# A two-layer hybrid decoder trunk: weight squares between an output group's high parts, squares behind the third tile's copies at the layer boundary, and another hand-written order for the first tiles

## The chip, the cores and the metric

One core of a Trainium2 chip. The metric is the device time of one execution in microseconds (us). TensorE (PE) multiplies matrices; VectorE (DVE), ScalarE (ACT) and GpSimd (POOL) do the rest; SyncE (SP) issues most DMA transfers.

## The reference

Two layers; the input is 512 tokens of width 2048 in float32. Each layer normalises, projects once to all branches, runs three branches and projects their concatenation back:

```python
def _layer(x, norm_g, w_in, conv_w, conv_b, sb_qn_g, sb_kn_g, gla_w_up, gla_b_up, gla_on_g, w_out):
    h = _rmsnorm(x, norm_g).astype(x.dtype)
    proj = h @ w_in
    (cv_h, cv_b, cv_c, cv_g, sb_q, sb_k, sb_v, sb_g,
     gl_q, gl_k, gl_v, gl_g, gl_lr) = jnp.split(proj, split_points, axis=-1)
    y_conv = _short_conv(cv_h, cv_b, cv_c, conv_w, conv_b) * jax.nn.silu(cv_g.astype(f32))
    ...  # y_sb: stick-breaking attention on q, k, v; y_gla: gated linear attention in chunks of 64
    mix = jnp.concatenate([y_conv, y_sb, y_gla], axis=-1).astype(x.dtype)
    return x + mix @ w_out
```

`w_in` is 2048 x 7696 and `w_out` 2048 x 2048 in each layer, both float32. The changed places belong to `_rmsnorm` and `h @ w_in` (the first tiles and the layer boundary) and to `x + mix @ w_out` (the output groups).

## The kernel before

**Numbers in two parts.** Every float32 operand of a product is scaled by a power of two and split into two float16 parts, a high one and a low one (what the high one left), and a product is three matmuls: high by high, high by low, low by high. The activations are `mix`, two constant tiles (`act` in the rows), 128 rows by 16 slices of the width by 4 token tiles.

**Weight groups.** Weights are worked on in groups of 256 columns; the list `specs` has them in the order of use, and `i` is a group's place in it. For each group:
- `fetch` (L332 issues the DMAs on SP) brings two staged float32 halves, `st`, of 1 MB each. There are four such buffers, so two groups are staged at a time.
- `wmax` takes the sum of squares of each half on ACT (L344, 128x2048, result into `wm`, kept in the dictionary `peak`; the instruction in `squares`).
- `wscale` sums over the partitions on POOL (L357, into `wgm`) and works out the scale on DVE (L359 to L371, `ws` the scale, `wu` its inverse). POOL and these DVE steps run only once the second square is there.
- Either `whi`/`wlo` write four quarters, a high part on ACT (L419, with L417 for a group that has 16 more columns) and a low part on DVE (L423); or, where `modes[i]` is set, `right` writes the seven right operands of a two-by-two product with seven instead of eight block products: seven high parts on ACT (L436) and seven low parts on DVE (L437), and between them four DVE sums of staged blocks (L440, L441, L444, L445), for which later high parts wait. The result tiles are `w`, of which the pool has six.
- `weights()` hands a group to its user, issues `fetch(i + 2)` and calls `load(i + 1)`, so a group is prepared while the one before it is multiplied.

In `load_` the two squares of group i are put, in ACT's order, behind the second high part of group i - 1. `tc.issue_after(x)` is a hint for the scheduler: the enclosed instructions stand behind x in their engine's queue. Everything else outside the hand-written stretch is placed by a scheduler that simulates the kernel; `tc.high_priority()` moves work ahead of what else is ready. The instructions of each engine are then run in that order.

**Output groups.** `w_out` has eight groups in each layer. In layer 0, groups 2 to 6 go through `seven`, group 7 through `project_by_token` (matmuls L653); in layer 1, groups 2 to 7. `seven` multiplies seven products of 48 matmuls each (L680, 128x128), of which the first needs the first high and low part of the group, the second the second and so on (product order 0, 1, 3, 2, 4, 5, 6). Its results are combined on ACT (L691) and DVE (L1380 to L1402) with the residual, and in layer 0 ACT squares them for the next layer's norm (`square`, L1348).

**The first tiles.** Up to L620 or so the order of DVE and ACT is written by hand (`tc.manual_schedule`): the lines of calls stand in the order in which both engines run them. For each of four token tiles of 128 rows: `xsquare` (ACT, L547) sums the squares of its input; `xnorm` works out the factor (L198, L199 on ACT, L201 to L205 and L495 on DVE); `xgain` multiplies (DVE, L501, one for each half); `xhigh` transposes eight 128x128 blocks on PE (L513) and copies the result as the high part (ACT, L515); `xlow` makes the low part, either by a DVE subtract (L522) or by two PE matmuls with the negative identity (L525) and a copy on ACT (L526). Group 0's quarters are `whi0` (high parts: ACT L407 or DVE L409) and `wlo` (L423). PE's first products (L653) use the first tiles as they come.

**The layer boundary.** The last output group of layer 0 is done by token tile, and each finished tile goes straight into layer 1's preparation, `xprep`: tiles 0 and 1 by split copies and transposing transfers on SP, tiles 2 and 3 by `xhigh` and `xlow`. In the same stretch the first weight groups of layer 1 are prepared.

Of the kernel before, what the change touches and what calls it, by code (L numbers as in the profile page):

```python
# [10 lines left out]
AF = mybir.ActivationFunctionType  # L11
# [28 lines left out]
def hybrid_trunk(ctx, tc, x, norm_g, w_in, conv_w, conv_b, sb_qn_g, sb_kn_g,  # L40
# [3 lines left out]
    depth, D = norm_g.shape  # L44
# [28 lines left out]
    def sm(n, tag, bufs=None):  # L73
        return small.tile([P, n], F32, tag=tag, name=nm(tag), bufs=bufs)
# [117 lines left out]
        V.tensor_scalar(c.bitcast(I32), c.bitcast(I32), 0x7F800000, None, ALU.bitwise_and)  # L192
        V.tensor_scalar(dst, c, 2.0 ** lift, None, ALU.mult)

    def rsqrt(dst, src, scale, n, tag):

        r0 = sm(n, tag + "r0")
        S.activation(r0, src, AF.Ln, scale=scale, bias=epst)  # L198
        S.activation(r0, r0, AF.Exp, scale=-0.5)  # L199
        m = sm(n, tag + "rm")  # L200
        V.tensor_scalar(m, src, scale, EPS, ALU.mult, ALU.add)  # L201
        t = sm(n, tag + "rt")
        V.scalar_tensor_tensor(t, r0, -0.5, r0, ALU.mult, ALU.mult)
        V.tensor_tensor(t, t, m, ALU.mult)
        V.scalar_tensor_tensor(dst, t, 1.5, r0, ALU.add, ALU.mult)  # L205

    identb = const.tile([P, P], BF16, tag="identb", name="identb")
    V.tensor_copy(identb, ident)
# [81 lines left out]
    specs = []  # L290
# [49 lines left out]
    def wmax(i, h):  # L340

        if h == 0:
            peak[i] = sm(2 + len(specs[i][2]) // 2, "wm")
        squares[i] = S.activation(junk(HK * GW).rearrange("p (k n) -> p k n", k=HK), staged[i][h], AF.Square,  # L344
                                  accum_out=peak[i][:, h:h + 1])
        if h and len(specs[i][2]) > 1:
            S.activation(junk(KT * LR).rearrange("p (k n) -> p k n", k=KT), staged[i, 2], AF.Square,
                         accum_out=peak[i][:, 2:3])
# [53 lines left out]
    def whi0(h, q, eng):  # L402

        wtile(0)
        hi = quarter(0, 2 * h + q, 0)
        if eng is S:
            S.activation(hi, staged4(0, 2 * h + q), AF.Copy, scale=scales[0])  # L407
        else:
            V.tensor_scalar(hi, staged4(0, 2 * h + q), scales[0], None, ALU.mult)  # L409
# [18 lines left out]
    def right(i):  # L428

        a, b = (staged[i][0][:, :, c * P:(c + 1) * P] for c in range(2))  # L430
        c, d = (staged[i][1][:, :, c * P:(c + 1) * P] for c in range(2))

        def part(x):
            w = wtile(i)
            hi, lo = (w[:, h, :HK * P].rearrange("p (k n) -> p k n", n=P) for h in range(2))
            his.setdefault(i, []).append(S.activation(hi, x, AF.Copy, scale=scales[i]))  # L436
            V.scalar_tensor_tensor(lo, x, scales[i], hi, ALU.mult, ALU.subtract)  # L437

        part(a)
        V.tensor_tensor(b, b, d, ALU.add)  # L440
        V.tensor_tensor(a, a, b, ALU.add)  # L441
        part(a)
        part(c)
        V.tensor_tensor(c, c, a, ALU.add)  # L444
        V.tensor_tensor(a, a, d, ALU.subtract)  # L445
        part(a)
        part(b)
        part(d)
        part(c)

    def load_(i):

        with tc.issue_after(his[i - 1][min(1, len(his[i - 1]) - 1)].ins):
            for h in range(2):
                wmax(i, h)
        wscale(i)
        if modes[i]:
            right(i)
            return
        for q in range(4):  # L460
            whi(i, q)
            wlo(i, q)
# [23 lines left out]
    def xnorm(l, t):  # L486

        tot = ssq[:, t, 0:1]
        if l:
            tot = sm(1, "xtot")  # L490
            V.tensor_reduce(tot, ssq[:, t, :], AX.X, ALU.add)
        rstd = sm(1, "xrstd")
        rsqrt(rstd, tot, 1.0 / D, 1, "x")
        rs_ = sm(1, "xrs")
        V.tensor_tensor(rs_, rstd, xsc[:, l:l + 1], ALU.mult)  # L495
        xscale[t] = rs_
# [6 lines left out]
            V.scalar_tensor_tensor(xv[:, n:], tail[0][:, t, :], xscale[t], gb[h][:, n:], ALU.mult, ALU.mult)  # L503

    xps = {}

    def xhigh(t, h, dst):

        xv = xt[t // 2][:, t % 2, :]
        xps[t, h] = ps = bank2().rearrange("p a (k c) -> p (a k) c", c=P)  # L510
        for i in range(HK):
            k = h * HK + i
            T.matmul(ps[:, i, :], xv[:, k * P:(k + 1) * P], ident, start=i % 4 == 0, stop=True, is_transpose=True,  # L513
                     skip_group_check=True)
        S.activation(dst[0][:, h * HK:(h + 1) * HK, t, :], ps, AF.Copy)  # L515

    def xlow(t, h, dst, on_pe):

# [27 lines left out]
    def xsquare(t):  # L546
        S.activation(junk(D), xt[t // 2][:, t % 2, :], AF.Square, accum_out=ssq[:, t, 0:1])  # L547
# [9 lines left out]
    wpeak0(2)  # L557
    wpeak0(1)
    xhigh(0, 0, mix)
    xsquare(1)  # L560
    wscale(0)
    whi0(0, 0, S)
    whi0(0, 1, V)
    xhigh(0, 1, mix)
    whi0(1, 0, V)
    xnorm(0, 1)
    whi0(1, 1, S)
    xgain(1, 0)
    xgain(1, 1)
    xlow(0, 0, mix, True)  # L570
    xlow(0, 1, mix, True)
    for q in range(4):
        wlo(0, q)
    xhigh(1, 0, mix)
    xhigh(1, 1, mix)
    xsquare(2)
    xlow(1, 0, mix, False)
    xlow(1, 1, mix, False)
    xnorm(0, 2)
    xgain(2, 0)  # L580
    xgain(2, 1)
    xsquare(3)
    xnorm(0, 3)
    xhigh(2, 0, mix)
    xhigh(2, 1, mix)
    wmax(1, 0)
    xgain(3, 0)
    xgain(3, 1)
    xlow(2, 0, mix, False)
    xlow(2, 1, mix, False)  # L590
    wmax(1, 1)
    wscale(1)
# [871 lines left out]
```

## Time and profile before

| | |
|---|---|
| median of three runs | 1666.27 us (1665.41 to 1667.84) |
| profiled execution | 1664.92 us, span 1663.0 us |
| mean granted TensorE clock | 0.999 |
| busy PE / weight loads / DVE / ACT / POOL | 1633.4 / 1344.6 / 1432.1 / 1249.0 / 72.5 us |
| memory traffic | 117 GB/s over the span |

A row of a timeline reads: start, duration, engine, line, operation, output<-inputs, shape, count, and in brackets the idle time just before on that engine with what ended it. A row of waits reads: engine, what waited, what it waited for, total us, times, longest. A row of windows reads: the stretch and its length, then for PE, weight loads, DVE, ACT and POOL the busy time (and instruction count), then the granted clock, the share of the DMA engines and GB/s. Rows of the same line with many instructions are merged (x48).

### The profile page before, as it was taken

What the parts mean: (1) busy time and instruction counts of PE and PEld (TensorE: products, weight loads), DVE (VectorE), ACT (ScalarE), POOL (GpSimd) and SP (SyncE); (2) the same over time, 40 slices, a digit from 0 to 9 for tenths busy, and PEclk for the clock granted to TensorE, in tenths of its full rate; (3) what the DMA queues carried; (4) which work ended last, traced back from release to release, by engine and by line L of the source; (5) the groups of instructions that cost most, each with busy time, mean ns of one, the idle gap of its engine ahead of it and who ended that gap; (6) DMA issues with size and microseconds to landing.
All of it is one profiled execution on the core that took longest, in us unless ns stands there. A gap on an engine that the chain in (4) does not pass through costs nothing.

```text
span 1663.0 us, 40940 instructions
## 1 busy us (share of the span) xinstructions
PE 1633.4 (98%) x17594; PEld 1344.6 (81%) x17594; DVE 1432.1 (86%) x2346; ACT 1249.0 (75%) x1721; POOL 72.5 (4%) x96
## 2 busy tenths in 40 slices
PE   7999999999999999999999999999999999999999
PEld 5755748998999986799986657588989898858999
DVE  7987888899898987988788788988999998979886
ACT  8878777696978788567776778776969696976653
POOL 0110000000000000000001000000000000000000
PEclk9999999999999999999999999999999999999999
DMA  8563331446363649255658424224564546473441
GB/s 261 134 162 110 102 121 58 128 101 163 96 168 104 157 127 283 61 168 162 217 139 187 118 77 134 95 84 109 139 136 126 149 121 155 131 234 99 154 154 52
DMA packets 308100, 227.60 MB, mean 137 GB/s; under 512 B 127650, under 2 KB 301004, under 8 KB 307408
## 3 DMA queue, kind: packets, MB, share of 16 engines
q1 hardware_dynamic: 298912, 215.55, 47.1%
q10 hardware_dynamic: 9008, 9.45, 1.8%
q8 instruction: 137, 2.24, 0.6%
q14 instruction: 43, 0.35, 0.1%
HBM read 179.88 MB, written 14.68 MB: 117 GB/s over the span
## 4 chain that ended last, share of the span: by engine, by line
PE 25%; DVE 13%; issue 8%; ACT 6%; DMA 3%; SPq 1%; POOL 1%; ACTq 0%; DVEq 0%; POOLq 0%
PE psp L680 6%; PE psp L677 6%; DVE w L437 3%; PE psp L653 2%; ACT w L436 2%; PE psp L643 2%; PE psp L642 2%; PE psp L641 2%; ACT junk L344 2%; DMA st<-in_w_out_dram 1%; PE psp L625 1%; PE psp L627 1%; PE psp L626 1%; DMA st<-in_w_in_dram 1%; DVE w L423 1%
## 5 line engine op out<-in xcount | busy, mean ns | idle before, releaser
L436 ACT ACTIVATE w<-st,ws 128x1024 f16<-128x1024 f32 x287 | 321.3, 1141 | 153.9 <-DVE st L441 66.3
L437 DVE SCALAR_TENSOR_TENSOR w<-st,ws,w 128x1024 f16<-128x1024 f32 x287 | 362.7, 1280 | 69.3 <-ACT w L436 66.3
L344 ACT ACTIVATE junk<-st 128x2048 uint8<-128x2048 f32 x150 | 284.9, 1899 | 22.3 <-DMA st<-in_w_in_dram 15.7
L677 PEld LDWEIGHTS <-w 128*128 128x128 f16 x2688 | 262.3, 98 | 36.9 <-issue 3.9
L642 PE MATMUL psp<-w,act 128*128 128x256 f16 x896 | 244.0, 273 | 0.0
L641 PE MATMUL psp<-w,act 128*128 128x256 f16 x896 | 243.8, 273 | 0.0
L643 PE MATMUL psp<-w,act 128*128 128x256 f16 x896 | 243.7, 273 | 0.0
L680 PE MATMUL psp<-w,act 128*128 128x128 f16 x3600 | 215.3, 219 | 7.1 <-DVE raw L731 3.2
L680 PEld LDWEIGHTS <-act 128*128 128x128 f16 x3600 | 205.3, 98 | 11.1 <-issue 6.1
L625 PE MATMUL psp<-act,w 128*128 128x512 f16 x512 | 194.0, 379 | 0.0
L626 PE MATMUL psp<-act,w 128*128 128x512 f16 x512 | 194.0, 379 | 0.0
L627 PE MATMUL psp<-act,w 128*128 128x512 f16 x512 | 194.0, 379 | 0.0
L423 DVE SCALAR_TENSOR_TENSOR w<-st,ws,w 128x1024 f16<-128x1024 f32 x140 | 177.6, 1279 | 18.0 <-ACT w L419 17.6
L677 PE MATMUL psp<-s,w 128*128 128x256 f16 x1536 | 176.9, 273 | 2.2 <-DVE vv L723 1.9
L419 ACT ACTIVATE w<-st,ws 128x1024 f16<-128x1024 f32 x136 | 153.4, 1140 | 27.9 <-PE psp L627 14.8
L680 PE MATMUL psp<-w,s 128*128 128x128 f16 x2688 | 156.3, 219 | 0.8 <-DVE vv L723 0.7
L680 PEld LDWEIGHTS <-s 128*128 128x128 f16 x2688 | 152.0, 98 | 2.4 <-issue 2.3
L677 PE MATMUL psp<-act,w 128*128 128x256 f16 x1152 | 135.0, 273 | 0.0
L357 POOL PARTITION_ALL_REDUCE wgm<-wm x75 | 56.2, 750 | 1429.0 <-ACT junk L344 1298.5
L653 PE MATMUL psp<-w,act 128*128 128x256 f16 (+1 forms) x960 | 111.5, 277 | 4.6 <-ACT w L407 2.2
L653 PEld LDWEIGHTS <-act 128*128 128x128 f16 x960 | 94.0, 98 | 20.2 <-issue 3.1
L625 PEld LDWEIGHTS <-w 128*128 128x128 f16 x512 | 50.1, 98 | 58.4 <-issue 0.7
(358 smaller groups left out, 2655.3 us busy)
## 6 DMA issues: line engine op xcount, KB each, us to landing
st<-in_w_in_dram SPq DMA_DIRECT2D x120, 1024.0 KB, 6.1
st<-in_w_out_dram SPq DMA_DIRECT2D x32, 1024.0 KB, 5.8
m<-mixd SPq DMA_DIRECT2D x24, 256.0 KB, 5.4
x<-in_x_dram SPq DMA_DIRECT2D x4, 1024.0 KB, 11.9
qT<-in_x_dram ACTq DMA_DIRECT2D x8, 512.0 KB
qT<-xs ACTq DMA_DIRECT2D x8, 512.0 KB, 3.9
out_dram<-kT SPq DMA_DIRECT2D x16, 256.0 KB, 2.1
mixd<-e SPq DMA_DIRECT2D x12, 256.0 KB
```

Source lines behind the costliest of these rows:

```text
L344: squares[i] = S.activation(junk(HK * GW).rearrange("p (k n) -> p k n", k=HK), staged[i][h], AF.Square, accum_out=peak[i][:, h:h + 1])
L436: his.setdefault(i, []).append(S.activation(hi, x, AF.Copy, scale=scales[i]))
L437: V.scalar_tensor_tensor(lo, x, scales[i], hi, ALU.mult, ALU.subtract)
L625: T.matmul(o, wh, xh[:, k, :, :], start=st_, stop=False)
L626: T.matmul(o, wh, xl[:, k, :, :], start=False, stop=False)
L627: T.matmul(o, wl, xh[:, k, :, :], start=False, stop=en)
L641: T.matmul(o, xh[:, k, t, :], wh, start=k == 0 and t % 2 == 0, stop=False, skip_group_check=True)
L642: T.matmul(o, xh[:, k, t, :], wl, start=False, stop=False, skip_group_check=True)
L643: T.matmul(o, xl[:, k, t, :], wh, start=False, stop=k == lastk, skip_group_check=True)
L653: T.matmul(o[:, :n], a_[:, k, t, :], wview(w, part, k, n), start=i == 0 and k == 0, stop=i == 2 and k == KT - 1)
L677: T.matmul(o[:, :2 * P], ww, x[xi][:, k, :, :], start=first, stop=final, skip_group_check=True)
L680: T.matmul(o[:, t * P:(t + 1) * P], x[xi][:, k, t, :], ww, start=first, stop=final, skip_group_check=True)
```

## The change

It touches the order in three places; two matmuls and one copy take the place of one subtract, and otherwise no work is added or taken away.

1. In `right`, where group i and the one two before it both belong to `w_out` (and i is not the last group), the two squares of group i + 1 stand behind the second and third high parts of group i, and the last four high parts of group i stand behind those squares. `load_` then skips its squares for a group that has them.
2. In `load_`, for layer 1's third weight group, the squares stand behind the second copy of token tile 2 (`copies[2, 1]`) instead of behind the second high part of the group before.
3. In the hand-written order: the first tile's second half is copied before the second tile's square; all four high parts of group 0 are made on DVE; the second tile's first low part goes through PE and ACT instead of DVE; the norm is split into `xnorma` and `xnormb`, and the third tile's square stands ahead of the second tile's copies, the fourth tile's ahead of the second tile's low parts.

Lines after the change are 8 to 40 higher: L436 is L447 (the first three high parts) or L450 (those with the hint), L437 is L451, L344 is L352, L1348 is L1388, L515 is L551, L522 is L558, L526 is L562, L547 is L583, L407 and L409 are L415 and L417, L419 is L427, L843 is L883, L691 is L731.

```diff
...
@@ -430,10 +438,16 @@
         a, b = (staged[i][0][:, :, c * P:(c + 1) * P] for c in range(2))
         c, d = (staged[i][1][:, :, c * P:(c + 1) * P] for c in range(2))
 
+        behind = None
+
         def part(x):
             w = wtile(i)
             hi, lo = (w[:, h, :HK * P].rearrange("p (k n) -> p k n", n=P) for h in range(2))
-            his.setdefault(i, []).append(S.activation(hi, x, AF.Copy, scale=scales[i]))
+            if behind is None:
+                his.setdefault(i, []).append(S.activation(hi, x, AF.Copy, scale=scales[i]))
+            else:
+                with tc.issue_after(behind.ins):
+                    his[i].append(S.activation(hi, x, AF.Copy, scale=scales[i]))
             V.scalar_tensor_tensor(lo, x, scales[i], hi, ALU.mult, ALU.subtract)
 
         part(a)
@@ -441,6 +455,11 @@
         V.tensor_tensor(a, a, b, ALU.add)
         part(a)
         part(c)
+        if specs[i][1] is w_out and specs[i - 2][1] is w_out and modes[i] and i + 1 < len(specs):
+            for h in range(2):
+                with tc.issue_after(his[i][h + 1].ins):
+                    wmax(i + 1, h)
+            behind = squares[i + 1]
         V.tensor_tensor(c, c, a, ALU.add)
         V.tensor_tensor(a, a, d, ALU.subtract)
         part(a)
@@ -450,9 +469,14 @@
 
     def load_(i):
 
-        with tc.issue_after(his[i - 1][min(1, len(his[i - 1]) - 1)].ins):
-            for h in range(2):
-                wmax(i, h)
+        l = specs[i][0]
+        if i not in peak:
+            behind = his[i - 1][min(1, len(his[i - 1]) - 1)]
+            if l and specs[i - 2][1] is w_in and specs[i - 3][1] is w_out:
+                behind = copies[2, 1]
+            with tc.issue_after(behind.ins):
+                for h in range(2):
+                    wmax(i, h)
         wscale(i)
         if modes[i]:
             right(i)
@@ -489,8 +513,19 @@
         if l:
             tot = sm(1, "xtot")
             V.tensor_reduce(tot, ssq[:, t, :], AX.X, ALU.add)
+        xnorma(t, tot)
+        xnormb(l, t)
+
+    seeds = {}
+
+    def xnorma(t, tot=None):
+
+        seeds[t] = rsqrt_seed(ssq[:, t, 0:1] if tot is None else tot, 1.0 / D, 1, "x")
+
+    def xnormb(l, t):
+
         rstd = sm(1, "xrstd")
-        rsqrt(rstd, tot, 1.0 / D, 1, "x")
+        rsqrt_step(rstd, *seeds.pop(t), 1, "x")
         rs_ = sm(1, "xrs")
         V.tensor_tensor(rs_, rstd, xsc[:, l:l + 1], ALU.mult)
         xscale[t] = rs_
@@ -503,6 +538,7 @@
             V.scalar_tensor_tensor(xv[:, n:], tail[0][:, t, :], xscale[t], gb[h][:, n:], ALU.mult, ALU.mult)
 
     xps = {}
+    copies = {}
 
     def xhigh(t, h, dst):
 
@@ -512,7 +548,7 @@
             k = h * HK + i
             T.matmul(ps[:, i, :], xv[:, k * P:(k + 1) * P], ident, start=i % 4 == 0, stop=True, is_transpose=True,
                      skip_group_check=True)
-        S.activation(dst[0][:, h * HK:(h + 1) * HK, t, :], ps, AF.Copy)
+        copies[t, h] = S.activation(dst[0][:, h * HK:(h + 1) * HK, t, :], ps, AF.Copy)
 
     def xlow(t, h, dst, on_pe):
 
@@ -557,36 +593,40 @@
     wpeak0(2)
     wpeak0(1)
     xhigh(0, 0, mix)
+    xhigh(0, 1, mix)
     xsquare(1)
     wscale(0)
-    whi0(0, 0, S)
+    whi0(0, 0, V)
     whi0(0, 1, V)
-    xhigh(0, 1, mix)
     whi0(1, 0, V)
+    whi0(1, 1, V)
     xnorm(0, 1)
-    whi0(1, 1, S)
     xgain(1, 0)
     xgain(1, 1)
     xlow(0, 0, mix, True)
     xlow(0, 1, mix, True)
-    for q in range(4):
-        wlo(0, q)
+    wlo(0, 0)
+    wlo(0, 1)
+    wlo(0, 2)
+    wlo(0, 3)
+    xsquare(2)
     xhigh(1, 0, mix)
     xhigh(1, 1, mix)
-    xsquare(2)
-    xlow(1, 0, mix, False)
+    xnorma(2)
+    xsquare(3)
+    xlow(1, 0, mix, True)
+    xnormb(0, 2)
     xlow(1, 1, mix, False)
-    xnorm(0, 2)
     xgain(2, 0)
     xgain(2, 1)
-    xsquare(3)
-    xnorm(0, 3)
+    xnorma(3)
+    xnormb(0, 3)
     xhigh(2, 0, mix)
     xhigh(2, 1, mix)
     wmax(1, 0)
     xgain(3, 0)
+    xlow(2, 0, mix, False)
     xgain(3, 1)
-    xlow(2, 0, mix, False)
     xlow(2, 1, mix, False)
     wmax(1, 1)
     wscale(1)
```

The part left out splits `rsqrt` into `rsqrt_seed` (the two ACT steps L198, L199 and DVE's `m`) and `rsqrt_step` (the three DVE steps), which `xnorma` and `xnormb` call.

ACT in layer 0's output projection, before: the last four high parts of one `seven` group (scale `ws_10037`), the squares of the next group (`junk`, `wm`), and that group's first three high parts (scale `ws_10445`); `ssq` rows are squares of results.

```order
L436 ACTIVATE w_10054<-st_9772,ws_10037 128x1024
L436 ACTIVATE w_10057<-st_9772,ws_10037 128x1024
L436 ACTIVATE w_10060<-st_9774,ws_10037 128x1024
L436 ACTIVATE w_10063<-st_9774,ws_10037 128x1024
L344 ACTIVATE junk_10437,wm_10436<-st_10024 128x2048
L344 ACTIVATE junk_10439,wm_10436<-st_10026 128x2048
L1348 ACTIVATE junk_10829,ssq_9524<-x_9522 128x256
L436 ACTIVATE w_10449<-st_10024,ws_10445 128x1024
L1392 ACTIVATE nu_11132<-wu_10447 128x1
L1348 ACTIVATE junk_10831,ssq_9524<-x_9522 128x256
L436 ACTIVATE w_10454<-st_10024,ws_10445 128x1024
L436 ACTIVATE w_10457<-st_10026,ws_10445 128x1024
```

After, the same group (now scale `ws_10447`): its first three high parts, the squares of the group behind it (`st_10439`, `st_10441`), and three of its last four.

```order
L447 ACTIVATE w_10451<-st_10031,ws_10447 128x1024
L1388 ACTIVATE junk_10435,ssq_9526<-x_9525 128x256
L447 ACTIVATE w_10456<-st_10031,ws_10447 128x1024
L447 ACTIVATE w_10459<-st_10033,ws_10447 128x1024
L352 ACTIVATE junk_10463,wm_10462<-st_10439 128x2048
L352 ACTIVATE junk_10465,wm_10462<-st_10441 128x2048
L1388 ACTIVATE junk_10836,ssq_9526<-x_9524 128x256
L1388 ACTIVATE junk_10838,ssq_9526<-x_9524 128x256
L450 ACTIVATE w_10469<-st_10031,ws_10447 128x1024
L450 ACTIVATE w_10472<-st_10031,ws_10447 128x1024
L450 ACTIVATE w_10475<-st_10033,ws_10447 128x1024
```

The squares have moved from between two groups into the middle of the group ahead of theirs, and the last four high parts of that group stand behind them.

ACT at the layer boundary, before: two quarters of a group of layer 1 (`w_12451`, `w_12456`), squares of the next group (`junk`, `wm_12683`), and between them the copies of token tiles 2 and 3 (`act_183<-psz`).

```order
L419 ACTIVATE w_12451<-st_12048,ws_12447 128x4x256
L417 ACTIVATE w_12456<-ga_12052,ws_12447 128x4x16
L419 ACTIVATE w_12456<-st_12048,ws_12447 128x4x256
L344 ACTIVATE junk_12684,wm_12683<-st_12431 128x2048
L515 ACTIVATE act_183<-psz_12311 128x8x128
L515 ACTIVATE act_183<-psz_12324 128x8x128
L843 ACTIVATE v_12428<-psp_12522 128x256
L344 ACTIVATE junk_12686,wm_12683<-st_12433 128x2048
L515 ACTIVATE act_183<-psz_12403 128x8x128
L515 ACTIVATE act_183<-psz_12416 128x8x128
```

After:

```order
L427 ACTIVATE w_12453<-st_12050,ws_12449 128x4x256
L425 ACTIVATE w_12458<-ga_12054,ws_12449 128x4x16
L427 ACTIVATE w_12458<-st_12050,ws_12449 128x4x256
L551 ACTIVATE act_183<-psz_12313 128x8x128
L551 ACTIVATE act_183<-psz_12326 128x8x128
L352 ACTIVATE junk_12686,wm_12685<-st_12433 128x2048
L883 ACTIVATE v_12430<-psp_12524 128x256
L352 ACTIVATE junk_12688,wm_12685<-st_12435 128x2048
L551 ACTIVATE act_183<-psz_12405 128x8x128
L551 ACTIVATE act_183<-psz_12418 128x8x128
```

The two copies of tile 2 have moved ahead of the first square.

ACT among the first tiles, before: the high parts of the first tiles (`act_183`), the low parts through PE (`act_184`), squares of the input (`junk_221`, `junk_295`), two high parts of group 0 (`w_233`, `w_261`).

```order
L515 ACTIVATE act_183<-psz_211 128x8x128
L547 ACTIVATE junk_221,ssq_182<-x_87 128x2048
L407 ACTIVATE w_233<-st_163,ws_229 128x1024
L515 ACTIVATE act_183<-psz_237 128x8x128
L198 ACTIVATE xr_43_250<-ssq_182,epst 128x1
L199 ACTIVATE xr_43_250<-xr_43_250 128x1
L407 ACTIVATE w_261<-st_165,ws_229 128x1024
L526 ACTIVATE act_184<-psz_211 128x8x128
L526 ACTIVATE act_184<-psz_237 128x8x128
L515 ACTIVATE act_183<-psz_275 128x8x128
L515 ACTIVATE act_183<-psz_285 128x8x128
L547 ACTIVATE junk_295,ssq_182<-x_88 128x2048
```

After:

```order
L551 ACTIVATE act_183<-psz_211 128x8x128
L551 ACTIVATE act_183<-psz_221 128x8x128
L583 ACTIVATE junk_231,ssq_182<-x_87 128x2048
L198 ACTIVATE xr_43_251<-ssq_182,epst 128x1
L199 ACTIVATE xr_43_251<-xr_43_251 128x1
L562 ACTIVATE act_184<-psz_211 128x8x128
L562 ACTIVATE act_184<-psz_221 128x8x128
L583 ACTIVATE junk_275,ssq_182<-x_88 128x2048
L551 ACTIVATE act_183<-psz_277 128x8x128
L551 ACTIVATE act_183<-psz_287 128x8x128
```

Group 0's high parts have left ACT, the second copy of tile 0 has moved ahead of the square of tile 1, and the square of tile 2 ahead of the copies of tile 1.

More of the change, by code (lines that the diff above doesn't have):

```diff
@@ L193, in pow2, with rsqrt_seed @@
         V.tensor_scalar(dst, c, 2.0 ** lift, None, ALU.mult)
-    def rsqrt(dst, src, scale, n, tag):
+    def rsqrt_seed(src, scale, n, tag):
         r0 = sm(n, tag + "r0")
@@ L201, in rsqrt, with rsqrt_step @@
         V.tensor_scalar(m, src, scale, EPS, ALU.mult, ALU.add)
+        return r0, m
+    def rsqrt_step(dst, r0, m, n, tag):
         t = sm(n, tag + "rt")
@@ L205, in rsqrt @@
         V.scalar_tensor_tensor(dst, t, 1.5, r0, ALU.add, ALU.mult)
+    def rsqrt(dst, src, scale, n, tag):
+        rsqrt_step(dst, *rsqrt_seed(src, scale, n, tag), n, tag)
     identb = const.tile([P, P], BF16, tag="identb", name="identb")
```

## Prediction

> **What bounds the kernel now.** I read the page's busy shares first, then TensorE's idle time by what ended it, then busy time by stage, then the stages that the change touches row by row.
>
> ```profile
> PE 1633.4 (98%) x17594; PEld 1344.6 (81%) x17594; DVE 1432.1 (86%) x2346; ACT 1249.0 (75%) x1721; POOL 72.5 (4%) x96
> PE psp L680 <- DVE w L437: 3.6, 4, 1.1
> PE psp L653 <- ACT w L407: 2.2, 1, 2.2
> ACT w L436 <- DVE st L441: 66.3, 36, 5.5
> 0.00:40.00 40.00, 31.00 (x202) 22.87 (x203) 31.35 (x89) 32.64 (x45) 1.22 (x8) 0.96 0.84 270
> 40.00:180.00 140.00, 140.00 (x939) 88.07 (x937) 120.47 (x245) 109.64 (x163) 11.28 (x14) 1.00 0.47 121
> 722.00:824.00 102.00, 97.99 (x1707) 96.79 (x1705) 87.16 (x117) 73.94 (x113) 3.48 (x5) 1.00 0.58 181
> 1547.00:1640.00 93.00, 91.57 (x1632) 91.08 (x1630) 83.66 (x111) 55.35 (x62) 2.30 (x4) 1.00 0.46 147
> ```
>
> TensorE (PE) is the bound: 98% busy, at a granted clock of 1.00 (the column behind POOL's). A moved instruction can therefore only win time where PE stands idle, and 1663.0 - 1633.4 = 29.6 us is all there is of that. The stage rows (length, then PE, weight loads, DVE, ACT, POOL) place it: 9.0 us in the first 40, none from 40 to 180, 4.0 in layer 0's output projection (722 to 824), 1.4 in layer 1's. The waits (total, times, longest) name what the change touches: PE waits for low parts of weights (L437) and high parts (L407), and ACT with its high parts (L436) waits 66.3 us in all for DVE's sums (L441).
>
> **Layer 0's output groups.** Each group is seven products of 48 matmuls; a product without a wait takes 725.43 - 722.75 = 2.68 us, so a dense group 18.76.
>
> ```profile
> 722.75 2.84 PE L680 MATMUL psp<-w,act 128*128 128x128 f16 x48
> 725.43 2.84 PE L680 MATMUL psp<-w,g 128*128 128x128 f16 x48
> 746.98 4.27 ACT L436 ACTIVATE w<-st,ws 128x1024 f16<-128x1024 f32 x4
> 751.15 1.89 ACT L344 ACTIVATE junk<-st 128x2048 uint8<-128x2048 f32 x1
> 753.17 1.91 ACT L344 ACTIVATE junk<-st 128x2048 uint8<-128x2048 f32 x1
> 755.27 0.41 POOL L357 PARTITION_ALL_REDUCE wgm<-wm  x1 [19.67 <-ACT junk L344]
> 756.59 0.14 DVE L369 TENSOR_SCALAR ws<-wq 128x1 int32<-128x1 f32 x1
> 757.18 1.13 ACT L436 ACTIVATE w<-st,ws 128x1024 f16<-128x1024 f32 x1
> 758.35 1.29 DVE L437 SCALAR_TENSOR_TENSOR w<-st,ws,w 128x1024 f16<-128x1024 f32 x1 [1.49 <-ACT w L436]
> 759.69 5.46 PE L680 MATMUL psp<-w,act 128*128 128x128 f16 x95 [1.10 <-DVE w L437]
> ```
>
> This is a serial chain at a group's start: the last four high parts of the old group, then 4.0 us of squares of the new one, then the sum over partitions, the scale, the first high part, the low part, and only then PE. The change puts the squares behind the old group's second and third high parts, where ACT otherwise waits for DVE's sums (the 66.3 us above), so the scale is known some 4 us before the first high part needs it, and this stall goes. The squares' 4 us are not new work. What could come late next is a later high part, since four of them now stand behind the squares.
>
> The price has three readings. Layer 1's groups already run in nearly the new order (its first such group changes by two swaps, worth 0 within 0.3), and PE's idle there is 1.43 us in 93, or 1.57 in 102; against 4.01 in layer 0 that leaves a gain of 2.4. The distance of one group's reduction from the next is longer by more:
>
> ```profile
> 715.18 0.41 POOL L357 PARTITION_ALL_REDUCE wgm<-wm  x1 [44.07 <-ACT junk L344]
> 814.69 0.46 POOL L357 PARTITION_ALL_REDUCE wgm<-wm  x1 [18.44 <-ACT junk L344]
> 1541.92 0.88 POOL L357 PARTITION_ALL_REDUCE wgm<-wm  x1 [29.08 <-ACT junk L344]
> 1618.27 0.58 POOL L357 PARTITION_ALL_REDUCE wgm<-wm  x1 [18.55 <-ACT junk L344]
> ```
>
> These are first and last of six and of five: 99.51 / 5 = 19.90 us a group in layer 0 and 76.35 / 4 = 19.09 in layer 1, so five groups gain 4.1. Third, the new order laid out by hand with the durations above keeps all but 0.5 us of the five groups dense, a gain of 4.6. I take 3.5, the middle of 2.4 and 4.6. Below 2.4 it goes only by the second rival's way.
>
> [...] The two rows of weight loads above give 5.21 idle in 102 and 1.92 in 93, so a gain of 3.1 instead of 2.4; with 3.1 as the term the whole sum below would be 6.0 instead of 6.4.
>
> **The prologue.**
>
> ```profile
> 14.70 1.91 ACT L547 ACTIVATE junk<-x 128x2048 uint8<-128x2048 f32 x1
> 15.52 1.41 DVE L409 TENSOR_SCALAR w<-st,ws 128x1024 f16<-128x1024 f32 x2
> 18.97 1.13 ACT L407 ACTIVATE w<-st,ws 128x1024 f16<-128x1024 f32 x1
> 19.87 2.48 DVE L501 SCALAR_TENSOR_TENSOR x<-x,xrs,g 128x1024 f32<-128x1024 f32 x2
> 22.27 4.87 DVE L423 SCALAR_TENSOR_TENSOR w<-st,ws,w 128x1024 f16<-128x1024 f32 x4
> 27.05 2.35 DVE L522 TENSOR_TENSOR act<-psz,act 128x1024 f16<-128x1024 f32 x2
> 30.46 2.48 DVE L501 SCALAR_TENSOR_TENSOR x<-x,xrs,g 128x1024 f32<-128x1024 f32 x2
> 38.26 1.09 PE L513 MATMUL psz<-ident,x 128*128 128x128 f32 x8 [1.83 <-DVE act L522]
> 46.77 1.90 ACT L344 ACTIVATE junk<-st 128x2048 uint8<-128x2048 f32 x1
> 48.90 1.14 ACT L419 ACTIVATE w<-st,ws 128x1024 f16<-128x1024 f32 x1
> 50.18 1.14 ACT L419 ACTIVATE w<-st,ws 128x1024 f16<-128x1024 f32 x1
> ```
>
> Laid out by hand, in the new order: all four high parts of group 0 on DVE (0.7 each) end at 18.2 instead of two on ACT that end at 20.1. On ACT the second copy now stands ahead of the second tile's square, which ends at 17.7 instead of 16.7, yet the norm's small steps follow it at once, and the gains begin at 19.0 (19.87 before). The gains, the low parts and one subtract instead of two (1.2 less on DVE; the other half goes to two more matmuls of PE and a copy on ACT, both idle here) bring the third tile's gains to 28.4 (30.46), and its subtracts, on which PE's fourth-tile transposes wait 1.83, end some 2 us sooner. PE stands 2.0 to 2.5 earlier at 40 us. Part is given back: the second group's third and fourth high parts stay behind the third group's squares (the last three rows). I lay these two to end at 48.75 and 50.05, while PE, earlier by 2.3, wants them at 48.1 and 49.7: about 1 us. So I take 1.5, what the rows laid out give, with 0 (all given back) and 2.5 (nothing) as bounds; a loss is excluded, since no high part of the second group ends later than now.
>
> **The layer boundary.**
>
> ```profile
> 844.94 6.50 PE L653 MATMUL psp<-w,act 128*128 128x256 f16 x58 [0.78 <-DMA act<-raw]
> 854.43 1.89 ACT L344 ACTIVATE junk<-st 128x2048 uint8<-128x2048 f32 x1
> 856.33 1.91 ACT L515 ACTIVATE act<-psz 128x1024 f16<-128x1024 f32 x2
> 857.38 1.96 PE L653 MATMUL psp<-w,act 128*128 128x256 f16 x16 [1.35 <-ACT act L515]
> ```
>
> With the squares behind the third tile's copies, those copies begin at 854.4 instead of 856.33, and PE's 1.35 goes, since 1.9 is more than 1.35. The first square then ends about 2 us later, but the second, and the reduction behind it, only by the pieces' changed order, under 1 us; that weight group is wanted by PE well behind the present one, so I see no loss. The 0.78 waits for a transposing transfer; the first token tile's finish (L1360) moves ahead of a low part of 1.3, which can only bring that forward. I take 1.4, bounds 0 and 2.1. The remaining moves (some DVE and ACT rows near 110 us, two swaps on SP) lie in a stretch where PE has no idle time (140.00 of 140.00), which hides them: 0.
>
> **Sum.** 3.5 + 1.5 + 1.4 = 6.4. The profiled execution has 1664.92, so 1658.5; its distance to the median is 1.35, so about 1660 against 1666.27. Nothing that follows is tied to a fixed time, so an earlier start carries to the end.
>
> **Rivals.** 0.2% of this kernel, 3.3 us, is about what its measurement can tell from no change.
>
> *No change that can be told.* The prologue's gain is given back whole at the second group, layer 0 gets its 2.4 or less, the boundary's stall turns into one for the squares' scale. That is 1 to 3 us, about 1664. For it speaks that PE is at 98% and that the stretch of 40 to 180 can take back a lead; against it that three separate stalls are addressed. 0.20.
>
> *Slower.* ACT takes its instructions in order. If a group's squares stand in front of its weights' landing, four high parts of the old group stand behind them. The nearest rows:
>
> ```profile
> 1589.36 7.55 DMA st<-in_w_out_dram
> x<-in_x_dram SPq DMA_DIRECT2D x4, 1024.0 KB, 11.9
> ```
>
> In layer 1 the chain of work goes through such a landing (7.55), and no PE idle follows from it. By my layout the squares have about 1 us beyond that. The rival begins at a landing of 8.5, and has eaten the change's whole gain at 9.9, where five groups lose 5 x 1.4 = 7.0, the 4.0 they lose now and the other 2.9 gained; at 11, on the way to the first load's 11.9, they lose 12.5, which is 5.6 slower: 1672. [...] 0.08.
>
> *All dense.* Every bound at its far end: 4.6 + 2.5 + 2.1 = 9.2, so 1657. 0.10. The forecast itself has 0.62.
>
> **Range and chances.** 1656.5 to 1666.0: from the dense case to the gains' lower bounds (2.4 + 0 + 0 is 1664) and the measurement's 2 us beyond. Faster by over 0.2%: 0.62 + 0.10; within: 0.20; slower: 0.08.
>
> **What the changed profile would show.** Layer 0: reductions 19.1 us apart or less, the long PE waits on the first low part gone, and ACT's squares with no wait on a landing. Prologue: PE's eight transposes of the fourth tile's first half some 2 us earlier and a new short wait of PE on high parts at 46 to 50. Boundary: no wait on the third tile's copy. The forecast is wrong if the squares on ACT show waits on transfers in layer 0 (slower), or if the lead at 45 us is gone by 60 us.

## The result and the profile after

| | before | after |
|---|---|---|
| median of six runs | 1666.25 us (1665.41 to 1667.84) | 1658.43 us (1657.43 to 1660.82) |
| profiled execution / span | 1664.92 / 1663.0 us | 1658.41 / 1656.4 us |

The ratio is 0.9955, with a 95% interval of 0.9944 to 0.9966, so 7.5 us faster, with 5.7 and 9.3 as its ends (the two medians differ by 7.8). The forecast was 1660.0, and the likeliest case came. The first view is again the stages, then what TensorE (PE) waited for, for the kernel after (lines are those of the changed kernel):

```profile
PE 1632.7 (99%) x17596; PEld 1343.5 (81%) x17596; DVE 1431.7 (86%) x2347; ACT 1247.4 (75%) x1720; POOL 73.1 (4%) x96
0.00:40.00 40.00, 33.01 (x225) 24.08 (x226) 32.49 (x94) 32.12 (x45) 1.50 (x8) 1.00 0.84 271
720.00:822.00 102.00, 101.94 (x1751) 100.76 (x1749) 88.81 (x124) 78.04 (x119) 6.39 (x6) 1.00 0.62 198
1540.00:1633.00 93.00, 92.38 (x1650) 92.02 (x1647) 83.63 (x111) 54.81 (x60) 2.15 (x4) 1.00 0.46 147
PE psp L717 <- ACT kT L963: 0.9, 1, 0.9
PE psz L549 <- DVE act L558: 0.5, 1, 0.5
```

PE's busy time is the same (1632.7 against 1633.4); the span lost idle time. Layer 0's output projection went from 4.0 us idle in 102 to 0.06, the first 40 us from 9.0 to 7.0 (before's 31.00 busy there holds a stretch at a lower granted clock, 0.53 and 0.79 in two slices, see the first tiles below). The last two rows are new or longer waits, at 933 and at the layer boundary, where leads were given back.

How far the kernel is ahead at each place is read from a landmark that both profiles have, such as the start of the n-th sum over partitions on POOL. Two rows of after, and the row of before that the second answers to (its 715.18 stands in the prediction):

```profile
713.02 0.41 POOL L365 PARTITION_ALL_REDUCE wgm<-wm  x1 [44.05 <-ACT junk L352]
818.62 0.41 POOL L365 PARTITION_ALL_REDUCE wgm<-wm  x1 [21.38 <-ACT junk L352]
```

```profile
825.60 0.41 POOL L357 PARTITION_ALL_REDUCE wgm<-wm  x1 [10.44 <-ACT junk L344]
```

The lead is 715.18 - 713.02 = 2.2 us ahead of the output groups of layer 0 and 825.60 - 818.62 = 7.0 behind them: 4.8 us were won there. Table of leads against the profile of before, in us, by the same landmarks (their times in before):

| profile | 161 | 715 | 826 | 908 | 953 | 1206 | 1439 | 1618 |
|---|---|---|---|---|---|---|---|---|
| after | 1.7 | 2.2 | 7.0 | 6.9 | 6.8 | 6.8 | 5.4 | 6.6 |
| out_only | -0.5 | -0.2 | 4.6 | 4.3 | 4.6 | 4.5 | 2.3 | 1.2 |
| first_only | 1.2 | 1.8 | 1.8 | 1.3 | 1.2 | 1.1 | 0.6 | 1.1 |
| bound_only | -0.5 | 0.5 | 0.5 | 0.8 | 0.5 | -1.5 | -2.2 | -2.4 |
| lows_later | 1.1 | 2.3 | 7.0 | 7.0 | 6.5 | 4.8 | 2.4 | 3.5 |

The rows other than the first are the experiments below. Two kernels with the same first tiles differ by up to 0.6 at 161 (the two parts that leave them alone stand at -0.5), and behind 953 by 1 to 3.4: that is what one profile's lead is worth as a reading. A difference taken inside one row, over a short stretch, is much steadier.

### The profile page after: what moved, and what is told of

The parts are those of the page before. It is cut to its first block, busy times and chain, and to the rows that moved or that the text cites. A ratio compares the mean times of both kernels' runs of the same rounds, so it can differ in the third digit from the quotient of the medians.

```text
span 1656.4 us, 40941 instructions
## 1 busy us (share of the span) xinstructions
PE 1632.7 (99%) x17596; PEld 1343.5 (81%) x17596; DVE 1431.7 (86%) x2347; ACT 1247.4 (75%) x1720; POOL 73.1 (4%) x96
## 3 DMA queue, kind: packets, MB, share of 16 engines
q8 instruction: 137, 2.24, 0.6%
## 4 chain that ended last, share of the span: by engine, by line
PE 17%; DVE 13%; issue 12%; ACT 4%; DMA 3%; SPq 1%; POOL 1%; ACTq 0%; DVEq 0%; POOLq 0%
PE psp L720 4%; DVE w L451 3%; PE psp L717 3%; PE psp L682 1%; PE psp L683 1%; PE psp L681 1%; DMA st<-in_w_out_dram 1%; DVE w L431 1%; PE psp L665 1%; PE psp L667 1%; PE psp L666 1%; DMA st<-in_w_in_dram 1%; ACT w L447 1%; SPq L829 1%; PE psp L693 1%
## 5 line engine op out<-in xcount | busy, mean ns | idle before, releaser
L451 DVE SCALAR_TENSOR_TENSOR w<-st,ws,w 128x1024 f16<-128x1024 f32 x287 | 362.6, 1280 | 62.2 <-ACT w L447 54.2
L447 ACT ACTIVATE w<-st,ws 128x1024 f16<-128x1024 f32 x247 | 277.5, 1141 | 140.7 <-DVE st L455 75.4
L352 ACT ACTIVATE junk<-st 128x2048 uint8<-128x2048 f32 x150 | 284.9, 1900 | 25.5 <-DMA st<-in_w_in_dram 18.8
L431 DVE SCALAR_TENSOR_TENSOR w<-st,ws,w 128x1024 f16<-128x1024 f32 x140 | 177.9, 1279 | 18.4 <-ACT w L427 18.0
L427 ACT ACTIVATE w<-st,ws 128x1024 f16<-128x1024 f32 x136 | 153.6, 1141 | 29.2 <-PE psp L667 14.6
```

## The experiments

**The parts alone.** Each is the kernel before with one part of the change.

out_only (`right`, and in `load_` only the skip):

```diff
+        if i not in peak:
-        with tc.issue_after(his[i - 1][...].ins):
+            with tc.issue_after(his[i - 1][...].ins):
```

> The kernel before with the output groups' part of the change alone (squares of the next group behind the second and third high part of a group, the last four high parts behind them). Theory A, each part removes its own waits of TensorE and the gains add: the five stalls of layer 0's output groups go (4.0 us idle in 722 to 824 down to under 0.3), the lead at the first reduction behind the output groups is 4.8 us, at the end about 4.5, so some 1661.7 us and a ratio of 0.997. Rival B, the parts need each other (the output groups gain only since layer 0's earlier parts start sooner): a lead under 3 us. Rival C, part of the gain is made in layer 1's last groups, whose first group's order changes by two swaps: idle in layer 1's groups falls from 1.4 to about 0.6 here too, by this part alone.

Measured: 1660.70 us against 1666.36, ratio 0.9971 (0.9961 to 0.9982), so 4.8 us faster (3.0 to 6.5). Its windows row over the output groups of layer 0:

```profile
722.00:824.00 102.00, 101.81 (x1750) 100.64 (x1749) 88.82 (x123) 78.22 (x120) 6.25 (x6) 1.00 0.63 198
```

0.2 us idle, and 4.8 us of lead between 715 and 826, as much as in the whole change. Theory A holds, B falls. C is not borne out: layer 1's groups have the new order in this kernel, and PE's waits there were 2.8 us in sum; in the whole change they were 0.6. Those waits vary from one execution to another; this profile loses 3.4 us of its lead behind 953, at a mean granted clock of 1.000 (before, with one drop, has 0.999).

first_only (the hand-written order alone; `right` and `load_` as before):

> The kernel before with the first tiles' new hand-written order alone. Theory A: TensorE's last transposes of the fourth tile end 2.3 us earlier, 1.7 us are left at 70 us and about 1.5 at the end, some 1664.7 us, not told from no change by time alone. Rival B (give-back): with no gain behind it the lead is eaten by later waits and at most 0.5 us is left at the end. Layer 0's output groups keep their 4 us of idle time.

Measured: 1665.33 us against 1666.36, ratio 0.9993 (0.9984 to 1.0002). By time alone nothing, as expected; by the landmarks 1.2 to 1.8 us of lead, 1.7 more than the two kernels that leave the first tiles alone at 161, and 1.1 at the end. Up to layer 0's output groups that is theory A; the 0.6 at 1439 and the 1.1 at the end lie between A's 1.5 and B's 0.5, so there one profile does not decide. Layer 0's output groups kept their waits (lead 1.8 on both sides).

bound_only:

```diff
+        behind = his[i - 1][...]
+        if l and specs[i - 2][1] is w_in and specs[i - 3][1] is w_out:
+            behind = copies[2, 1]
```

> The kernel before with the squares of layer 1's third weight group behind the third tile's second copy, and nothing else. Theory A: the wait of 1.35 us on the copy goes and a wait of about 0.5 us on the DVE subtract of that tile takes its place, so 0.7 us of lead at 865 us, and 0.2 to 0.7 at the end: no change by time. Theory of the prediction: no wait in its place, 1.35 us of lead. Rival D: the later squares hold back something in layer 1's middle, and nothing is left at 935 us.

Measured: 1666.61 against 1666.36, ratio 1.0005 (0.9996 to 1.0014): no change. The wait of 1.35 us on the copy is gone, and another stands at the next transposes:

```profile
857.98 1.09 PE L518 MATMUL psz<-ident,x 128*128 128x128 f32 x8 [0.73 <-DVE act L527]
```

**The new wait at the boundary.** lows_later is the changed kernel and

```diff
             whi(i, q)
-            wlo(i, q)
+            with tc.issue_after(lows[2, 1].ins):   # layer 1's second weight group only
+                wlo(i, q)
```

> The changed kernel with one more hint: at the layer boundary the four low parts of layer 1's second weight group stand on DVE behind the third tile's subtracts. If the new wait of 0.51 us is due to the two low parts (1.28 us each) that stand ahead of the subtracts on DVE, it goes and TensorE's fourth-tile transposes start 0.5 us earlier; the time falls by at most that, not told from the changed kernel (1658.4). If the subtract waits for the copy instead, the 0.51 stays, and the low parts come later by some 2.4 us without an effect, or with a new wait of TensorE for them.

Measured: 1660.42, ratio 0.9966 (0.9953 to 0.9978), not told from the changed kernel. The 0.51 us wait is gone, so it was the low parts ahead of the subtract on DVE. But at the next place where PE waited in after (0.86 us for kT) it now waited twice as long:

```profile
933.21 2.78 PE L722 MATMUL psp<-s,w 128*128 128x256 f16 x24 [1.77 <-ACT kT L968]
941.20 4.99 PE L722 MATMUL psp<-s,w 128*128 128x256 f16 x29 [1.87 <-DVE vv L768]
```

The profile's chain of work leads up to this place from a landing of weights, over squares, high parts and DVE's sums. The landing and the squares in it, in lows_later:

```profile
909.23 5.77 DMA st<-in_w_in_dram
915.08 2.00 ACT junk L352 x2
```

The half microsecond gained at the boundary is spent here (a lead of 7.0 at 908, 6.5 at 953). That the landing is what sets kT is read from the chain and was not tried.

**Which part of the new first-tile order counts.** xlow_dve is the changed kernel with `xlow(1, 0, mix, False)`, the second tile's first low part back on DVE.

> The changed kernel with the second tile's first low part back on DVE (a subtract) instead of PE and ACT. If that subtract (1.2 us of DVE) carries most of the first tiles' gain, TensorE's last transposes of the fourth tile start about 1.2 us later than in the changed kernel (37.7), and the lead at 70 us is 0.5 instead of 1.7 us. If the other moves carry it, under 0.4 us later.

Measured: 1660.76 us in its one run, 1658.41 the profiled one of the changed kernel. PE's last transposes of the fourth tile start at 41.18 instead of 37.72 (between the two timeline rows two rows of the windows, whose last columns are the granted clock, the DMA share and GB/s):

```profile
30.71 4.46 PE L693 MATMUL psp<-w,act 128*128 128x256 f16 x24 [1.53 <-DVE kg L285]
30.00:32.50 2.50, 1.79 (x10) 1.34 (x11) 2.50 (x4) 0.00 (x0) 0.00 (x0) 0.70 1.05 321
32.50:35.00 2.50, 2.50 (x16) 1.89 (x15) 1.44 (x14) 0.00 (x0) 0.00 (x0) 0.62 1.08 354
41.18 0.98 PE L549 MATMUL psz<-ident,x 128*128 128x128 f32 x7 [0.31 <-DVE act L558]
```

3.5 us later, not 1.2: the subtract pushed DVE's small steps back too, PE waited 1.53 for one of them, and the granted clock dropped behind that wait (0.70 and 0.62, so 2.5 x 0.30 + 2.5 x 0.38 = 1.7 us). Without the drop 1.8 are left, of the 2.3 us that the changed kernel gains at this place. At 161 its lead is -1.9, so about -0.2 without the drop, against 0 to -0.5 in the kernels with the old first tiles. So the low part through PE carries most of the first tiles' gain in this order, perhaps all of it, which is more than the 1.2 us of DVE that I had counted for it; this is one execution.

**Where the squares stand.** late_squares puts them behind the fourth and fifth high part (`his[i][h + 3]` in place of `his[i][h + 1]`, emitted behind `part(b)`).

> The changed kernel with the squares two high parts later: behind the fourth and fifth high part of a group, with only the last two high parts behind them. If what counts is that the scale is known before the next group's first high part, it is as fast as the changed kernel (lead over layer 0's output groups 4.5 to 5 us, no wait on a first low part). If it counts that the squares fill ACT's wait for DVE's sums, the last high parts come some 4 us later and waits on low parts of 0.5 to 1 us a group come back: a lead of 1 to 3 us.

Measured: 1661.77, ratio 0.9973 (0.9963 to 0.9984), 3 us behind the changed kernel. Idle in layer 0's groups is 2.35 us, and the wait is a new one, once in each of four groups:

```profile
722.00:824.00 102.00, 99.65 (x1714) 98.02 (x1712) 85.48 (x120) 75.62 (x118) 2.45 (x6) 1.00 0.61 191
751.03 0.28 PE L720 MATMUL psp<-w,raw 128*128 128x128 f16 x2 [0.58 <-DVE vv L1423]
```

No wait on a first low part: the scale is early enough here as well. What comes back is another wait, of PE for a result on DVE, with the products in another order, which the scheduler chose. Neither theory names it, though the lead it leaves (2.2 at 715, 4.5 at 908, so 2.3) falls into the second one's range; the gain does need more than an early scale.

**The rival that ends slower.** The first attempt added traffic: a 1 MB copy in memory ahead of each fetch of layer 0's output groups 3 to 7.

```diff
+            if src is w_out and not l and c0 >= 3 * GW:
+                nc.sync.dma_start(pad, src[l, ...])
```

> The changed kernel with more traffic: ahead of each staged half of layer 0's output groups 3 to 7 the same 1 MB is also copied from memory to a scratch place in memory on the same queue, so that the weights land later; the results do not change. In the changed kernel a fetch is issued at 747.5 and its squares start at 755.9 and 757.9, against a median landing of 6.1 us. Rival 'slower' of the prediction: the squares on ACT wait for the landing, four high parts stand behind them, and with a landing of 11 us or more each of five groups loses over 2.5 us: 12 us or more slower than the changed kernel, 1671 or more. Its opponent: the high parts behind the squares have slack of their own (ACT waits 3.8 us per group for a DVE sum), and the loss stays under 5 us.

> The kernel before with the same added traffic. There the squares start some 16 us after their fetch is issued (751.2 after 732.6 to 735.4), so a landing of 11 us costs nothing: within 1 us of 1666.3, if the landing of weights is all that the traffic delays. If both lose alike, it is the traffic and not the place of the squares.

Measured: 1695.15 (ratio 1.0176, 1.0161 to 1.0191) and 1702.16 (1.0216, 1.0199 to 1.0233). A miss, which tells nothing of the question: nothing in the program makes the copies wait, and the first tiles were late (34 and 35 us behind at the first landmark; in slow_before the fourth tile's transposes start at 73.77 instead of 38.26). That the copies ran at the very start and held the tiles back was the author's reading. In layer 0's output groups the profile shows no late weights, and the new order stays 7.0 us ahead of the old (1695.15 against 1702.16). It says only that the new order's 5 us are won from a start 34 us later too.

The second attempt makes the fetch itself late. Half a half is moved into the staged buffer first, then the right half over it:

```diff
+        if src is w_out and not l and c0 >= 3 * GW:
+            for h in range(2):
+                nc.sync.dma_start(tiles[h][:, :HK // 2, :], rows_[h][:, HK // 2:, :])
         for h in range(2):
             nc.sync.dma_start(tiles[h], rows_[h])
```

> The changed kernel with layer 0's output groups 3 to 7 fetched late: into each staged half 0.5 MB of other weights is moved first, then the right 1 MB over it, which waits for the first, on the same queue; results do not change. A half's landing should go from some 6 to 10 us, the second half's later still since the queue is held. In the changed kernel the squares follow the issue by some 8 us. Theory 'slower' of the prediction: squares wait on ACT for the landing, the four high parts behind them are late, TensorE waits for low parts again, 2 us or more per group, so 10 us or more over the changed kernel (1668 or more). Opponent: the high parts behind have slack (ACT waits 3.8 us a group for a DVE sum anyway), waits for the landing appear on ACT but under 3 us on TensorE in all.

> The kernel before with the same late fetches. Its squares start 16 us after the fetch is issued, so it should lose less than the changed kernel does: within 2 us of 1666.3. If it loses as much, the late weights are wanted by something else first (the sums on DVE, the high parts), and the place of the squares is not what makes the order sensitive.

Measured: 1680.39 us for the new order (ratio 1.0086, 1.0072 to 1.0100) and 1666.91 for the old (1.0003, 0.9994 to 1.0012). The late weights cost the new order 22 us and the old one nothing that can be told. Rows of ACT and one of PE, then the waits of 720 to 860, for the new order with late weights:

```profile
763.64 1.91 ACT L355 ACTIVATE junk<-st 128x2048 uint8<-128x2048 f32 x1 [2.54 <-DMA st<-in_w_out_dram]
771.09 1.91 ACT L355 ACTIVATE junk<-st 128x2048 uint8<-128x2048 f32 x1 [5.08 <-DMA st<-in_w_out_dram]
773.00 1.13 ACT L453 ACTIVATE w<-st,ws 128x1024 f16<-128x1024 f32 x1
774.18 0.27 PE L723 MATMUL psp<-w,zw 128*128 128x128 f16 x1 [4.24 <-DVE wu L382]
PE psp L723 <- DVE wu L382: 12.4, 4, 4.2
PE psp L723 <- DVE w L454: 2.2, 2, 1.1
ACT junk L355 <- DMA st<-in_w_out_dram: 26.7, 7, 5.6
DVE st L457 <- DMA st<-in_w_out_dram: 14.7, 3, 5.7
```

ACT's squares wait 26.7 us for landings, the high parts behind them come late, and PE waits 14.6 us. The profile puts 12.4 of these down to `wu`, which a product does not read; the first high part behind the squares ends at the same time (773.00 + 1.13, and PE starts at 774.18), and that one it reads. That is the rival's mechanism as it was put. It is not the only way in which the late weights reach PE: DVE's sum of the next group's blocks (L457) waits for the same landings with low parts behind it, 14.7 us in three waits, and the two were not separated. (The scheduler also shifted some squares of results on ACT in this kernel, which stand beside the moved ones.) The old order's profiled execution, its slowest at 1668.90, shows the late weights once: PE waits 2.25 us for a low part at 773.4, which stands on DVE behind a sum that waited for its landing, and the clock drops behind the wait. The median of the ten runs does not show it. The rest of the 22 us is the clock: four times it drops behind these waits, each time for about 1.7 us of work (the granted clock from 722 to 824 is 0.94 in the mean). The first of the four:

```profile
747.50:750.00 2.50, 0.00 (x0) 0.10 (x1) 1.57 (x5) 2.50 (x4) 0.41 (x1) 1.00 0.16 50
750.00:752.50 2.50, 2.38 (x23) 2.38 (x23) 2.48 (x4) 2.50 (x4) 0.00 (x0) 0.51 0.82 265
752.50:755.00 2.50, 2.50 (x40) 2.50 (x38) 2.50 (x4) 2.50 (x7) 0.00 (x0) 0.81 0.33 88
```

With a wait of 0.3 for one more high part, 14.6 + 0.3 + 4 x 1.7 = 21.7 of 22.0.

**A version that goes further.** vv_first takes the 1.87 us wait near 940 by its cause:

```diff
-        w, u = weights()
+        w, u = weights(late)          # does not prepare the next group yet
 ...
             ev.sub(vv, o3[:, :2 * P], u2)
+        if late:
+            load(i_ + 1)              # its low parts with issue_after(the subtract)
```

> The changed kernel with one subtract on DVE (vv of the seven-product group of layer 1's gated branch, for which TensorE waits 1.87 us near 940) ahead of a low part of the next weight group (1.28 us), by issuing that group's preparation behind it. If the low part and the two products ahead of it are what the subtract waits for, the 1.87 falls to 0.6 or less, and the drop of the granted clock that stood behind this wait in three of eight profiles (about 1.7 us each) does not come: 1.3 to 2 us faster than the changed kernel, some 1656.5. If the lead is taken back in the middle of layer 1, the end moves by less than 0.5 us.

Measured: 1657.27 us (1656.81 to 1658.17, five runs), ratio to before 0.9947 (0.9935 to 0.9960); the changed kernel's interval overlaps it, so that it beats the changed kernel is suggested and not shown. The wait fell less than expected:

```profile
938.69 0.49 PE L725 MATMUL psp<-s,w 128*128 128x256 f16 x3 [1.22 <-DVE vv L774]
```

0.65 us of the low part's 1.28 are won; other DVE work ahead of the subtract keeps 1.22. Its mean granted clock is 1.000, and the 47 matmuls behind this wait take 5.13 us (938.69 to 943.82), 0.109 each, as much as the 24 ahead of it (931.78 to 934.39).

## Why the prediction was right, and where not

- **Output groups: 3.5 forecast, 4.8 measured.** The mechanism holds, shown by the part alone and by the windows row. The size was taken between layer 1's idle (2.4) and the layout by hand (4.6), and the layout was right. Of the 4.8 us 3.9 were idle time (4.0 between these landmarks before, 0.07 after); the other 0.9 is PE's busy time for the same products, 106.4 before and 105.5 after, which the profile does not explain. The step that failed is the transfer from layer 1: PE's waits there are all on DVE results (L1396, 1.4 us in four waits), in layer 0 mostly on parts of weights (3.8 of 4.1), so layer 1 was no bound for what layer 0 can gain. The wait that the squares were to fill was misread as well. The 66.3 us for L441 stand in front of the second high part, so ahead of the squares' new place, and within this stage they grew, from 9.2 to 15.6 us; what went are ACT's waits for the scales, 8.8 us before and none after. The squares do stand where ACT would otherwise wait for a sum, but for the one of the fourth high part: in one group of after they end at 759.9, and that part starts at 761.8, after 0.75 us of waiting for the sum:

```profile
761.76 1.15 ACT L450 ACTIVATE w<-st,ws 128x1024 f16<-128x1024 f32 x1 [0.75 <-DVE st L464]
```

- **First tiles: 1.5 forecast, 1.7 measured.** The products behind the fourth tile's transposes start 2.3 us earlier (forecast 2.0 to 2.5) and 1.7 us are left at 70:

```profile
38.65 1.58 PE L693 MATMUL psp<-w,act 128*128 128x256 f16 x13
49.89 6.30 PE L693 MATMUL psp<-w,act 128*128 128x272 f16 x53 [0.19 <-ACT w L427]
69.78 0.38 PE L665 MATMUL psp<-act,w 128*128 128x512 f16 x1
```

  against these rows of before:

```profile
40.93 0.82 PE L653 MATMUL psp<-w,act 128*128 128x256 f16 x6
71.48 0.38 PE L625 MATMUL psp<-act,w 128*128 128x512 f16 x1
```

  The give-back was 0.6 and not 1.0: PE waited once for a high part, 0.19 us, near the place that I had named; the other 0.4 has no wait in the profile. One thing the prediction passed over: it took the granted clock as 1.00, but its own row of the first 40 us has 0.96. In before's profile the clock drops behind the wait of 2.2 for the high part (L407):

```profile
17.50:20.00 2.50, 2.21 (x10) 1.45 (x10) 0.76 (x5) 2.47 (x5) 0.00 (x0) 0.53 0.97 369
20.00:22.50 2.50, 2.50 (x19) 1.90 (x18) 2.50 (x3) 1.92 (x3) 0.00 (x0) 0.79 1.10 349
```

  That could have made the gain. It did not: out_only and bound_only have the same first tiles without a drop (mean granted clock 1.000 in out_only; 0.999 in bound_only, whose drop stands at 947.5 to 952.5) and are no earlier at 161 (-0.5). Which move earns it I had right in kind only: the low part through PE is worth more than its 1.2 us of DVE.
- **Boundary: 1.4 forecast, 0.8 at the place (1.35 of wait against 0.51), nothing at the end that the runs can tell.** This step failed. I had priced the wait on the copy as gone with nothing behind it. The DVE subtract behind the same copies stands in a queue with two low parts ahead of it, and PE waits 0.51 us for that (0.73 in bound_only). I had looked only at the engine on which the row moved. The leads agree: from 826 to 908 after goes from 7.0 to 6.9 and bound_only from 0.5 to 0.8, while the two parts without this move lose 0.3 and 0.5. In after, first PE, then DVE's low parts, whose line is L431, and last PE further on:

```profile
851.77 1.09 PE L549 MATMUL psz<-ident,x 128*128 128x128 f32 x8 [0.51 <-DVE act L558]
847.91 1.28 DVE L431 SCALAR_TENSOR_TENSOR w<-st,ws,w 128x1024 f16<-128x1024 f32 x1
849.30 1.28 DVE L431 SCALAR_TENSOR_TENSOR w<-st,ws,w 128x1024 f16<-128x1024 f32 x1
932.91 2.78 PE L717 MATMUL psp<-s,w 128*128 128x256 f16 x24 [0.86 <-ACT kT L963]
```

  What was left was spent at 932.91, on the chain from a landing (0.31 before). The wait of 0.78 on the transposing transfer stayed, 0.73.
- **"An earlier start carries to the end" was too simple.** In after, 7.0 at 826 became 6.6 at 1618, 5.4 in between; in other profiles 1 to 3.4 us went astray in layer 1, part of it on the clock. What is gained mostly carries, but layer 1's own waits vary by as much as the two smaller terms.
- **The rival "slower" was rightly put at a small chance**, for a reason that I had only estimated. In after, the squares start 8.4 and 10.4 us after the two halves' fetch and do not wait:

```profile
747.51 3.49 SPq L340 DMA_DIRECT2D st<-in_w_out_dram  x2
755.90 1.90 ACT L352 ACTIVATE junk<-st 128x2048 uint8<-128x2048 f32 x1
757.93 1.91 ACT L352 ACTIVATE junk<-st 128x2048 uint8<-128x2048 f32 x1
```

  Its condition, late weights, brings it about as described.
- **The sum.** 4.8 + 1.7 + 0 = 6.5, as against 6.4 forecast and 6.5 between the two profiled executions (1664.92 - 1658.41). Two terms were too small and one too large; that the total fits so well is partly luck. The runs say 7.5 (5.7 to 9.3), and the three parts alone add up to 4.8 + 1.2 - 0.8 = 5.2 by their runs; with intervals of some 1.5 us on either side of each, that neither shows nor excludes a gain beyond the sum.

The estimate of 3.1 for the first term, from the idle time of the weight loads, is nearer to the measured 4.8 than the 2.4 by matmuls; both lean on layer 1 and fall short for that. That ACT runs its instructions in their order is seen with the late weights: the high parts that stood behind the squares were late with them (773.00, right behind the square that had waited 5.08).

## What to carry to other kernels

Price a moved instruction on every engine that works on the same tile next, not only on the one where it moves: a wait that ends last hides the one that ends second (here 1.35 us on the copy hid 0.51 on the subtract), and that one is the price's lower end. Putting a statistic of the next block into the middle of this one wins where the engine idles there anyway, and it ties the order to the arrival of that block's data: test it once with the data made late. Lay the new order out by hand with measured durations rather than borrow a rate from another stage, unless the waits there have the same cause.

## What the runs showed of the hardware

A wait of PE of 1.87 us cost nearly twice its length in some of the profiles (1.87 + 1.7). Behind such waits the granted clock was lower, which is 1.7 us of lost work by the slices (0.51 and 0.81 in the two shown above; 2.5 x 0.49 + 2.5 x 0.19 = 1.7). In twice_before three matmuls inside the drop take 0.32 us (773.81 to 774.13), behind it 0.17 (777.23 to 777.40), and the slow ones last from 773.7 to 777.1, 3.4 us. The drop came behind all four groups of waits of twice_after (1.29 + 1.10 to 4.24 us), behind single waits of 2.24 (before), 2.25 (twice_before) and 2.00 (slow_before), and behind the same wait of 1.87 us near 940 in four of twelve profiles: twice_after, where 43 matmuls behind it take 6.52 us against 4.85 in before and after; late_squares (28 in 4.88) and lows_later (29 in 4.99); and bound_only, whose slices are:

```profile
945.00:947.50 2.50, 0.63 (x7) 0.42 (x5) 2.50 (x5) 2.50 (x3) 0.00 (x0) 1.00 0.83 237
947.50:950.00 2.50, 2.50 (x16) 1.88 (x15) 2.02 (x5) 2.50 (x6) 0.00 (x0) 0.59 0.66 200
950.00:952.50 2.50, 2.50 (x19) 1.95 (x18) 2.45 (x5) 2.50 (x4) 0.04 (x1) 0.72 0.98 326
```

That is 2.5 x 0.41 + 2.5 x 0.28 = 1.7, and most of the step from 0.5 at 953 to -1.5 at 1206 in its row of the table. In before the slices behind the waits of 1.06 (381.79), 1.35 (857.38), 1.44 (11.02), 1.83 (38.26) and 1.87 us (947.69) have a granted clock of 1.00, and so have those behind the 1.87 of after (940.90). How long a wait has to be is therefore not shown, and why the same wait drops the clock in some executions only was not tried. That runs of one kernel lie 1 to 3 us apart may be partly this.
